# The first chunk of four down projections computed with seven products instead of eight, and both such chunks at a new place among the pairs

## The chip, the cores and the metric

The kernel runs on one core of a Trainium2 chip. The metric is the device time of one execution in microseconds; smaller is better. Engines are called as in the profile: PE (TensorE matmul), PEld (its weight load), DVE (VectorE), ACT (ScalarE), POOL (GpSimd) and SP (SyncE, which here only issues DMAs).

## What is computed

A two-layer encoder on 512 tokens of width 1024, all in float32. Each layer is a gated feed-forward block, a mixer (attention of several kinds), a cross attention to a memory, and a second feed-forward block. The change touches the four feed-forward blocks alone (`ffn1` and `ffn2` of both layers):

```python
def swiglu(x, wg, wu, wd):
    return (jax.nn.silu(x @ wg) * (x @ wu)) @ wd

h = h + 0.5 * swiglu(rmsnorm(h, g), wg, wu, wd)      # wg, wu: 1024 x 2816, wd: 2816 x 1024
```

## The kernel before

Everything is held transposed: features on the 128 partitions, tokens along the free axis. The hidden width of 2816 is 22 blocks of 128, taken as 11 **pairs** of blocks, numbered 0 to 10. A float32 matrix product is made of three matmuls: each operand is parted into a high and a low float32r part (ACT writes the high part with a copy, DVE the low part with a subtraction), and high x high, high x low and low x high are summed in PSUM. "Operand" below is this pair of instructions (`operand`, lines 515 to 528; L526 is ACT's, L527 is DVE's).

**A pair's gate and up projections** are done with a seven-product scheme of Strassen and Winograd instead of eight quarter products (pair 0 alone is done plainly). The weights of a pair are four quarters of 128 x 1024 elements (512 KB); sums and differences of quarters, and of token halves, give seven products of 24 matmuls of 128 x 256 each. The names are those of the token sums they use: "11", "1", "2", "21", "3", "4" and "22". Four functions emit them:

- `open_pair` (L559): product 11, from quarter 0 (tile `wf`).
- `sum_pair` (L578): products 1 and 2. Their weights are made in tile `s1` (three buffers): one quarter is loaded from SP (L584), a second is added to it in flight by an accumulating DMA that POOL issues (L585), and DVE then subtracts quarter 0 (L591).
- `cross_pair` (L600): product 21 from quarter 1 (`wf`), then product 3. The weights of product 3 are made in tile `s3`, which has **one buffer**: SP loads a quarter (L614), ACT negates it (L616), POOL issues an accumulating DMA that adds another quarter (L617), then ACT and DVE make the operand. When DVE has made the low part, the buffer is free and the next load into it can be issued.
- `close_pair` (L625): products 4 (`lower`) and 22 (`upper`, whose DVE subtraction is L637), and the gate: two DVE multiplications (L670, L673), a Silu on ACT (L672), and the high and low parts of the hidden values (L436, L440).

The loop in `ffn` emits `sum_pair(p)`, `cross_pair(p)`, `open_pair(p+1)`, `close_pair(p)`, so that PE runs 1, 2, 21, 3 of pair p, 11 of pair p+1, and 4, 22 of pair p.

Operand buffers are few: two for `wh`/`wl`, and one pair `sh`/`sl` that every third operand uses. `wf` has three buffers.

**The down projection** goes over the hidden blocks in three chunks, `CHUNKS = (6, 8, 8)` blocks, that is pairs 0 to 2, 3 to 6 and 7 to 10. Its outputs are eight tiles of 128 x 512, kept in `f.sum`. Chunks 0 and 2 are plain (`down`, matmuls of 128 x 512 at L796): chunk 0 is emitted after `sum_pair(3)`, with eight weight loads of 384 KB, eight operands (L168, L170) and eight ACT copies into `f.sum` (L807). Chunk 1 is done with the seven-product scheme (`paired_down`, L703) after `cross_pair(7)`, in two halves (`s` = 0, 1) of seven products each, with its own tiles in the same buffers `wf`, `s1` and `s3` (L742 is the negation, L743 the accumulating DMA). It adds its results to `f.sum` with DVE (L710). What it needs of the hidden values, sums over token quarters, is made in the gate of each of its pairs (`hidden_sums`, L682: four subtractions at L686, and high and low parts at L695 and L696).

The gate of a pair is emitted at once, or put off until after the next pair's `sum_pair` (for p of 1, 2, 6 and 10).

PE's order is the order of the code. The order on the other engines is made by a scheduler when the kernel is built, with the operands at a high priority. Each queue, SP's and POOL's DMA issues among them, then runs strictly in that order.

Of the kernel before, what the change touches and what calls it, by code (L numbers as in the profile page):

```python
# [70 lines left out]
CHUNKS = (6, 8, 8)  # L71
PAIRED = 1

# [39 lines left out]
class Encoder:  # L113
    def __init__(self, tc, ctx, I):
        self.tc, self.nc, self.I = tc, tc.nc, I
        nc = self.nc
        pool = lambda name, bufs, **kw: ctx.enter_context(tc.tile_pool(name=name, bufs=bufs, **kw))
        self.const = pool("const", 1)
        self.xp = pool("xp", 1)
        self.wp = pool("wp", 2)  # L120
        self.ps = pool("ps", 4, space=PSUM)
        self.small = pool("small", 2)
        self.dram = pool("dram", 1, space=bass.MemoryType.DRAM)
        self.ident = self.const.tile([P, P], F32, name="ident")
        make_identity(nc, self.ident)
        self.identb = self.const.tile([P, P], BF, name="identb")
        nc.vector.tensor_copy(self.identb, self.ident)
# [10 lines left out]
        self.x = [None] * KB  # L138
        self.left = 0
# [43 lines left out]
    def xtile(self):  # L183
        return self.xp.tile([P, S], F32, name="x", tag="x", bufs=KB)

# [128 lines left out]
    def ffn(self, pre):  # L314


        with ExitStack() as ctx:
            pool = lambda name: ctx.enter_context(self.tc.tile_pool(name=pre + name, bufs=1))
            f = self.f = SimpleNamespace(pre=pre, ctx=ctx, hp=pool("h"), tp=pool("t"), H={}, n=0, taken=None, own=False, low=None, gate=None, spread=None, macc=None,
                                        G={n: [None] * (CHUNKS[PAIRED] // 2) for n in ("11", "21", "22", "1", "2", "3", "4")})  # L320
            R = self.plain_pair()
# [4 lines left out]
            for p in range(1, FB // 2):  # L326
                final = p == FB // 2 - 1
                self.sum_pair(pair)
                if f.gate is not None:
                    f.gate, gate = None, f.gate  # L330
                    gate(f.lowered)
                if p in ends and c != PAIRED:
                    self.down(c)
                    c += 1
                self.cross_pair(pair)
                if p == 2:
                    self.set_aside()
                if p in ends and c == PAIRED and p == ends[c]:
                    self.paired_down()
                    c += 1  # L340
                if final:
                    early = self.block(c, 0, True)
                    self.down_products(c, early, LEAD + REST, False)
                    self.close_pair(pair, True)
                    self.down(c, early)
                else:
                    old, pair = pair, self.open_pair(p + 1)
                    gate = self.close_pair(old, False)
                    if p <= 2 or p + 1 in ends:
# [69 lines left out]
    def hidden(self, p, gs, us):  # L419
# [95 lines left out]
    def operand(self, t, own=None):  # L515

        nc, f = self.nc, self.f
        if own is None:
            own = f.n % 3 == 2
            f.n += 1  # L520
        if own:
            h, l = self.own_tiles()
        else:
            h, l = [self.wp.tile([P, 1024 + WHOLE], F32R, name=n, tag=n, bufs=2)[:, o:o + 1024]
                    for n, o in (("wh", LINE), ("wl", LINE + STEP))]
        self.leading = nc.scalar.activation(h, t, AF.Copy)  # L526
# [11 lines left out]
    def raw_quarter(self, p, q):  # L538
        return self.fetch(self.wp.tile([P, 1024], F32, name="wf", tag="wf", bufs=3), p, q)

    def product(self, bank, w, xs, first, late=False):

        half = KB // 2
        ops = [(z, a, b, k) for z in range(2) for a, b in ((0, 0), (0, 1), (1, 0)) for k in range(half)]
        if late:
            ops.sort(key=lambda op: op[3] == half - 1)
        for n, (z, a, b, k) in enumerate(ops):
            o = z * 512 + k * P
            self.nc.tensor.matmul(bank[:, z * 256:z * 256 + 256], w[a][:, o:o + P], xs[k][b],  # L549
# [75 lines left out]
    def close_pair(self, pair, final):  # L625
# [40 lines left out]
        def gates(after=None):  # L666
# [6 lines left out]
            nc.vector.tensor_mul(two(gs), two(t), gu[:, :, 1, :])  # L673
            j = p - sum(CHUNKS[:PAIRED]) // 2
            if 0 <= j < CHUNKS[PAIRED] // 2:
                self.hidden_sums(p, j, gs, t)
            else:
                self.hidden_parts(p, gs, 0)

        return gates  # L680

    def hidden_sums(self, p, j, h, t):  # L682

# [6 lines left out]
        sub(part(t, 2), part(h, 2), part(t, 1))  # L690
        self.hidden_parts(p, h, 0)
        two = [f.hp.tile([P, S], F32R, name=n, tag="T", bufs=CHUNKS[PAIRED]) for n in ("th", "tl")]
        one = [self.xs[j][c][:, 256:512] for c in range(2)]
        for src, (hi, lo) in ((t[:, 0:512], two), (part(t, 2), one)):
            nc.scalar.activation(hi, src, AF.Copy)  # L695
            nc.vector.tensor_sub(lo, src, hi.bitcast(F32))  # L696
        whole = f.H[p]
        for name, tiles, i in (("11", whole, 0), ("1", whole, 1), ("21", whole, 2), ("22", whole, 3),
                               ("3", two, 0), ("2", two, 1)):
            f.G[name][j] = tuple(part(x, i) for x in tiles)  # L700
        f.G["4"][j] = tuple(one)

    def paired_down(self):  # L703

        nc, f = self.nc, self.f

        def add(s, b, half, bank):
            for z in range(2):
                o = f.sum[4 * s + 2 * b + z][:, half * 256:half * 256 + 256]
                nc.vector.tensor_add(o, o, bank[:, z * 256:z * 256 + 256])  # L710

        for s in range(2):
            p, late = -s, s == 0
            y = self.bank("pa")
# [13 lines left out]
            add(s, 1, 1, z)  # L728
            with self.tc.high_priority():
                nc.vector.tensor_sub(t, t, w11)  # L730
# [7 lines left out]
            add(s, 0, 0, x)  # L738
# [15 lines left out]
            self.product(y, w, f.G["4"], False)  # L754
            add(s, 1, 0, y)

    def set_aside(self):
# [10 lines left out]
        f.sum = [self.xtile() for _ in range(KB)]  # L768
        self.x = [None] * KB
# [30 lines left out]
    def down(self, c, first=None):  # L800
# [16 lines left out]
        if last:  # L817
            kept = []
            for d in range(KB):
                kept.append(f.hp.tile([P, S], F32, name="kept", tag="T", bufs=CHUNKS[PAIRED]))  # L820
                with self.behind(self.loaded):
# [580 lines left out]
    def mem_stats(self, p):  # L1402
# [370 lines left out]
def _layout(inp):  # L1773
# [28 lines left out]
    for l in (0, 1):  # L1802
        pre = "l%d_" % l
        for f in ("ffn1_", "ffn2_"):
# [62 lines left out]
```

## Time and profile before

| | us |
|---|---|
| median of three runs | 2036.51 (2034.72 to 2036.95) |
| the profiled execution | 2033.43 |
| its span in the trace | 2031.7 |
| PE busy | 2019.3 |
| DVE busy | 1531.1 |
| ACT busy | 1239.7 |
| POOL busy | 337.6 |

The four feed-forward blocks lie at about 9 to 346, 709 to 1038, 1038 to 1367 and 1698 to 2032 us of the span. In the rows of the trace a line is `engine line operation out<-in`; buffer numbers are left out, so both `s1` and `s3` read `s` there, and L617 or L743 tells `s3`, L585 or L725 `s1`. A matmul's own duration includes time in which the next one already runs, so the pace of PE is read from how many matmuls start in a stretch. The chain of waits is the chain of work that ended last, followed back from the end.

### The profile page before, as it was taken

The numbers are of one execution on the slowest core, as the hardware profiler recorded it, in microseconds if no ns is written. First come the engines' busy times: TensorE is split into PE (matmuls) and PEld (weight loads), VectorE is DVE, ScalarE is ACT, GpSimd is POOL, SyncE is SP. The second block draws the span as 40 slices with busy tenths as digits, with TensorE's granted clock in tenths as the row PEclk, the third lists the DMA queues.
The fourth block names the chain that finished last, engine by engine and source line by source line (L and its number), as shares of the span: only waits on it lengthen the run. The fifth ranks groups of instructions, "written<-read, shape, count | busy, mean of one in ns | idle before, by whom it ended". The sixth has DMA issues, their size and how long they took to land.

```text
span 2031.7 us, 34101 instructions
## 1 busy us (share of the span) xinstructions
PE 2019.3 (99%) x13421; PEld 1833.6 (90%) x13421; DVE 1531.1 (75%) x2285; ACT 1239.7 (61%) x1891; POOL 337.6 (17%) x321
## 2 busy tenths in 40 slices
PE   9999999999999999999999999999999999999999
PEld 7999998888888898999989999988888888999997
DVE  8679776799676794897677597864668688759784
ACT  7566564556785574665655565745768566656572
POOL 1021001345521110100010000003353111000000
PEclk9999999999999999999999999999999999999999
DMA  7667754222331185776456577644223324757762
GB/s 236 172 181 183 199 167 159 99 85 86 97 127 63 63 247 157 179 185 188 147 175 197 158 198 194 178 132 139 93 83 126 103 73 143 215 158 198 190 178 93
DMA packets 98800, 307.00 MB, mean 151 GB/s; under 512 B 11088, under 2 KB 14288, under 8 KB 98640
## 3 DMA queue, kind: packets, MB, share of 16 engines
q1 hardware_dynamic: 84528, 253.97, 37.6%
q0 software_dynamic: 13824, 50.34, 14.2%
q8 instruction: 105, 1.72, 0.3%
q10 hardware_dynamic: 288, 0.52, 0.1%
q14 instruction: 55, 0.45, 0.1%
HBM read 292.21 MB, written 12.58 MB: 150 GB/s over the span
## 4 chain that ended last, share of the span: by engine, by line
PE 94%; DVE 2%; DMA 1%; ACT 1%; issue 1%; POOL 0%; SPq 0%; DVEq 0%; ACTq 0%; POOLq 0%
PE ps_pa L549 30%; PE ps_pa L919 13%; PE ps_pb L549 12%; PE ps_pa L796 8%; PE ps_pb L796 8%; PE ps_pa L865 5%; PE ps_pa L393 3%; PE ps_pb L1032 3%; PE ps_pa L1522 2%; PE ps_pa L1353 2%; PE ps_pb L865 2%; PE ps_pb L1085 1%; PE ps_pb L1058 1%; PE ps_pb L393 1%; PE ps_pa L1252 1%
## 5 line engine op out<-in xcount | busy, mean ns | idle before, releaser
L168 ACT ACTIVATE wh<-wf 128x1024 fp32r<-128x1024 f32 (+2 forms) x187 | 181.6, 977 | 248.2 <-PE ps_pb L796 52.8
L170 DVE TENSOR_TENSOR wl<-wf,wh 128x1024 fp32r<-128x1024 f32 (+2 forms) x144 | 161.7, 1127 | 94.0 <-ACT wh L168 92.0
L527 DVE TENSOR_TENSOR wl<-s,wh 128x1024 fp32r<-128x1024 f32 x132 | 161.4, 1224 | 67.3 <-ACT wh L526 65.5
L526 ACT ACTIVATE wh<-s 128x1024 fp32r<-128x1024 f32 x132 | 140.0, 1062 | 107.2 <-PE ps_pa L549 31.1
L527 DVE TENSOR_TENSOR wl<-wf,wh 128x1024 fp32r<-128x1024 f32 x96 | 116.8, 1220 | 30.1 <-ACT wh L526 30.0
L617 POOL DMA_DIRECT2D s<-l_ffn_wq x40 | 34.9, 873 | 602.6 <-ACT s L616 345.0
L526 ACT ACTIVATE wh<-wf 128x1024 fp32r<-128x1024 f32 x96 | 101.4, 1059 | 50.7 <-PE ps_pa L549 22.1
L170 POOL TENSOR_TENSOR wl<-wf,wh 128x1024 fp32r<-128x1024 f32 (+1 forms) x43 | 95.0, 2209 | 185.6 <-ACT wh L168 123.4
L919 PE MATMUL ps_pa<-wh,xh 128*128 128x512 f32 x384 | 121.8, 398 | 0.0
L919 PE MATMUL ps_pa<-wh,xl 128*128 128x512 f32 x384 | 118.9, 391 | 0.0
L919 PE MATMUL ps_pa<-wl,xh 128*128 128x512 f32 x384 | 118.7, 390 | 0.0
L526 ACT ACTIVATE sh<-s 128x1024 fp32r<-128x1024 f32 x60 | 63.7, 1061 | 50.9 <-PE ps_pa L549 18.0
L527 DVE TENSOR_TENSOR sl<-s,sh 128x1024 fp32r<-128x1024 f32 x60 | 73.3, 1222 | 27.4 <-ACT sh L526 26.9
L919 PEld LDWEIGHTS ps_pa<-wh,xl 128*128 128x128 f32 x384 | 72.1, 188 | 15.7
L919 PEld LDWEIGHTS ps_pa<-wl,xh 128*128 128x128 f32 x384 | 72.0, 188 | 15.6
L1047 ACT ACTIVATE e<-e,m 128x128 f32<-128x128 f32 (+3 forms) x128 | 70.7, 554 | 21.6 <-DVE m L1046 21.4
L585 POOL DMA_DIRECT2D s<-l_ffn_wq x40 | 35.8, 895 | 285.4 <-DMA s<-l_ffn_wq 240.5
L919 PEld LDWEIGHTS ps_pa<-wh,xh 128*128 128x128 f32 x384 | 69.1, 188 | 12.5 <-DVE vp L964 0.3
L549 PE MATMUL ps_pa<-xh,wh 128*128 128x256 f32 x480 | 74.1, 276 | 0.0
L549 PE MATMUL ps_pa<-xl,wh 128*128 128x256 f32 x480 | 74.0, 276 | 0.0
L549 PE MATMUL ps_pa<-xh,wl 128*128 128x256 f32 x480 | 74.0, 276 | 0.0
L526 ACT ACTIVATE sh<-wf 128x1024 fp32r<-128x1024 f32 x48 | 50.8, 1059 | 36.5 <-PE ps_pa L549 16.9
(460 smaller groups left out, 6037.7 us busy)
## 6 DMA issues: line engine op xcount, KB each, us to landing
wf<-l_ffn_wq SPq DMA_DIRECT2D x120, 512.0 KB, 4.4
s<-l_ffn_wq SPq DMA_DIRECT2D x80, 512.0 KB, 4.3
s<-l_ffn_wq POOLq DMA_DIRECT2D x80, 512.0 KB, 7.6
wf<-l_w_in SPq DMA_DIRECT2D x48, 512.0 KB, 3.5
wf<-l_ffn_wd SPq DMA_DIRECT2D x32, 512.0 KB, 3.7
wf<-l_ffn_wd SPq DMA_DIRECT2D x32, 384.0 KB, 3.5
wf<-l_ffn_wdq SPq DMA_DIRECT2D x24, 512.0 KB, 4.5
s<-l_ffn_wdq SPq DMA_DIRECT2D x16, 512.0 KB, 4.0
```

Of the source, the lines that this page charges most:

```text
L168: self.leading = nc.scalar.activation(wh[:, sl], w[:, sl], AF.Copy)
L170: eng.tensor_sub(wl[:, sl], w[:, sl], wh.bitcast(F32)[:, sl])
L393: nc.tensor.matmul(p, w[a][:, k * P:(k + 1) * P], xs[k][c], start=k == order[0] and a == c == 0, stop=k == order[-1] and a == 1)
L526: self.leading = nc.scalar.activation(h, t, AF.Copy)
L527: self.parted = nc.vector.tensor_sub(l, t, h.bitcast(F32))
L549: self.nc.tensor.matmul(bank[:, z * 256:z * 256 + 256], w[a][:, o:o + P], xs[k][b], start=first and n == 0, stop=n == len(ops) - 1, skip_g ...
L796: self.nc.tensor.matmul(bank, w[a][:, j * P:(j + 1) * P], h, start=j == a == e == 0 and c < len(CHUNKS) - 1, stop=j == nb - 1 and (a, e) = ...
L865: nc.tensor.matmul(banks[dd], w[g, k // 2][a][:, o:o + P], parts(k)[b], start=k == first and a == b == 0, stop=k == last and a == 1)
L919: nc.tensor.matmul(banks[j], xs[k][a][:, j * P:(j + 1) * P], w[b][:, kk * 512:kk * 512 + 512], start=k == a == b == 0, stop=k == KB - 1 an ...
L1032: nc.tensor.matmul(bank[:, o:o + n], a, b[:, :n], start=c == 0, stop=c == len(ops) - 1)
L1047: nc.scalar.activation(e, e, AF.Exp, bias=m[:, i:i + 1], scale=-1.0, accum_out=rs[:, i:i + 1])
L1353: nc.tensor.matmul(banks[c][i], a[:, i * P:(i + 1) * P], b[:, c * 512:(c + 1) * 512], start=(k == 0 and n == 0), stop=(k == KB - 1 and n = ...
```

## The change

`PAIRED` becomes `(0, 1)`: chunk 0 is done by `paired_down` too, with matrices of 768 columns instead of 1024 and products of 18 matmuls of 128 x 256. Its first contribution to each output is copied by ACT instead of added by DVE; the other contributions, of both chunks, are added by one DVE instruction over two outputs, for which the tiles of `f.sum` become halves of tiles of 1024 columns. The hidden values of pairs 0, 1 and 2 now need the sums of `hidden_sums` too. `paired_down(c)` is no longer emitted after `cross_pair`, but one pair later, after `sum_pair` of the pair that follows: chunk 0 after `sum_pair(4)`, chunk 1 after `sum_pair(8)`. The gates that are put off are now those of pairs 1, 2, 3 and 7, and the gates of 3 and 7 come behind the paired chunk. In the last pair the operand of product 4 is put behind an operand of the last chunk.

```diff
-PAIRED = 1
+PAIRED = (0, 1)
...
     def xtile(self):
-        return self.xp.tile([P, S], F32, name="x", tag="x", bufs=KB)
+        if self.xroom is None:
+            self.xroom = self.xp.tile([P, 2 * S], F32, name="x", tag="x", bufs=KB // 2)
+            return self.xroom[:, :S]
+        room, self.xroom = self.xroom, None
+        return room[:, S:]
...
                 self.sum_pair(pair)
+                if c in PAIRED and p == ends[c] + 1:
+                    self.paired_down(c)
+                    c += 1
                 if f.gate is not None:
                     f.gate, gate = None, f.gate
                     gate(f.lowered)
-                if p in ends and c != PAIRED:
+                if p in ends and c not in PAIRED:
                     self.down(c)
                     c += 1
                 self.cross_pair(pair)
...
-                if p in ends and c == PAIRED and p == ends[c]:
-                    self.paired_down()
-                    c += 1
                 if final:
                     early = self.block(c, 0, True)
+                    f.ahead = self.leading
...
-                    if p <= 2 or p + 1 in ends:
+                    if p <= 2 or p in ends:
                         f.gate = gate
...
+    def hidden_done(self, p, h, t, later=False):
+
+        for c in PAIRED:
+            j = p - sum(CHUNKS[:c]) // 2
+            if 0 <= j < CHUNKS[c] // 2:
+                return self.hidden_sums(p, j, h, t, later)
+        self.hidden_parts(p, h, 0, later)
...
     def product(self, bank, w, xs, first, late=False):
 
-        half = KB // 2
+        half = len(xs)
...
-                w = self.operand(self.raw_quarter(p, 3), own)
+                w = self.raw_quarter(p, 3)
+                with self.behind(f.ahead):
+                    w = self.operand(w, own)
...
-    def paired_down(self):
+    def paired_down(self, c):
...
-        def add(s, b, half, bank):
-            for z in range(2):
-                o = f.sum[4 * s + 2 * b + z][:, half * 256:half * 256 + 256]
-                nc.vector.tensor_add(o, o, bank[:, z * 256:z * 256 + 256])
+        n = CHUNKS[c] * P
+
+        def add(s, b, half, bank, first=False):
+            o = self.halves(f.rooms[2 * s + b])[:, :, half * 256:half * 256 + 256]
+            if first and c == 0:
+                nc.scalar.copy(o, self.halves(bank))
+            else:
+                nc.vector.tensor_add(o, o, self.halves(bank))
...
-                t = f.tp.tile([P, 1024], F32, name="s1", tag="s1", bufs=3)
+                t = f.tp.tile([P, 1024], F32, name="s1", tag="s1", bufs=3)[:, :n]
...
-                v = f.tp.tile([P, 1024], F32, name="s3", tag="s3", bufs=1)
+                v = f.tp.tile([P, 1024], F32, name="s3", tag="s3", bufs=1)[:, :n]
```

Two places show what the scheduler made of it; both are in the second feed-forward block, and the other three blocks have the same order there. The first is SP's queue. Before, in the second half of the paired chunk 1 (its loads are those from `wdq`), up to the next load into the buffer `s3`:

```order
L535 DMA wf_10076<-l0_ffn2_wdq 128x1024
L535 DMA s3_10108<-l0_ffn2_wdq 128x1024
L535 DMA s1_10310<-l0_ffn2_wq 128x1024
L535 DMA wf_10173<-l0_ffn2_wdq 128x1024
L535 DMA wf_10206<-l0_ffn2_wq 128x1024
L535 DMA wf_10239<-l0_ffn2_wq 128x1024
L535 DMA s3_10402<-l0_ffn2_wq 128x1024
```

Now, in the second half of the paired chunk 0 (from `wdq0`):

```order
L550 DMA wf_9171<-l0_ffn2_wdq0 128x768
L550 DMA s3_9196<-l0_ffn2_wdq0 128x768
L550 DMA s1_9471<-l0_ffn2_wq 128x1024
L550 DMA wf_9247<-l0_ffn2_wdq0 128x768
L550 DMA wf_9291<-l0_ffn2_wq 128x1024
L550 DMA wf_9357<-l0_ffn2_wq 128x1024
L550 DMA s3_9322<-l0_ffn2_wq 128x1024
```

The two queues look alike, but what stands between the two `s3` products on PE differs: before, `s3_10402` belonged to pair 8, and products 22 and 4 of the chunk, 11 of pair 8, 4 and 22 of pair 7, and 1, 2 and 21 of pair 8 lay between; now `s3_9322` belongs to pair 4, whose product 3 comes after 22 and 4 of the chunk and 21 of pair 4.

The second place is DVE's queue in the same half. Before, from the subtraction for product 2 (L730) to the low part of the `s3` operand:

```order
L730 TENSOR_TENSOR s1_10012<-s1_10012,wf_9979 128x1024
L710 TENSOR_TENSOR x_8342<-x_8342,ps_pa_9751 128x256
L710 TENSOR_TENSOR x_8343<-x_8343,ps_pa_9751 128x256
L527 TENSOR_TENSOR sl_10047<-s1_10012,sh_10046 128x1024
L748 TENSOR_TENSOR s1_10012<-wf_10076,s1_10012 128x1024
L527 TENSOR_TENSOR wl_10079<-wf_10076,wh_10078 128x1024
L710 TENSOR_TENSOR x_8346<-x_8346,ps_pb_10011 128x256
L710 TENSOR_TENSOR x_8347<-x_8347,ps_pb_10011 128x256
L527 TENSOR_TENSOR wl_10113<-s3_10108,wh_10112 128x1024
```

Now, from the same subtraction (L765) to the low part of `s3_9196` and the low parts behind it:

```order
L765 TENSOR_TENSOR s1_9121<-s1_9121,wf_9094 128x768
L542 TENSOR_TENSOR wl_9149<-s1_9121,wh_9148 128x768
L542 TENSOR_TENSOR wl_9174<-wf_9171,wh_9173 128x768
L783 TENSOR_TENSOR s1_9121<-wf_9171,s1_9121 128x768
L655 TENSOR_TENSOR s1_8853<-wf_9291,s1_8853 128x1024
L542 TENSOR_TENSOR sl_9201<-s3_9196,sh_9200 128x768
L542 TENSOR_TENSOR wl_9225<-s1_9121,wh_9224 128x768
```

New in it is L655, the subtraction for product 22 of pair 4. It reads `wf_9291`, which takes the buffer of `wf_9094` that L765 was the last to read, and it stands ahead of the low part of the `s3` operand.

More of the change, by code (lines that the diff above doesn't have):

```diff
@@ L318, in ffn @@
             pool = lambda name: ctx.enter_context(self.tc.tile_pool(name=pre + name, bufs=1))
-            f = self.f = SimpleNamespace(pre=pre, ctx=ctx, hp=pool("h"), tp=pool("t"), H={}, n=0, taken=None, own=False, low=None, gate=None, spread=None, macc=None,
-                                        G={n: [None] * (CHUNKS[PAIRED] // 2) for n in ("11", "21", "22", "1", "2", "3", "4")})
+            f = self.f = SimpleNamespace(pre=pre, ctx=ctx, hp=pool("h"), tp=pool("t"), H={}, n=0, taken=None, own=False, low=None, gate=None, ahead=None, spread=None, macc=None,
+                                        G=[])
             R = self.plain_pair()
@@ L547, in product @@
         for n, (z, a, b, k) in enumerate(ops):
-            o = z * 512 + k * P
+            o = (z * half + k) * P
             self.nc.tensor.matmul(bank[:, z * 256:z * 256 + 256], w[a][:, o:o + P], xs[k][b],
@@ L673, in gates, with hidden_sums @@
             nc.vector.tensor_mul(two(gs), two(t), gu[:, :, 1, :])
[L674 to L678, printed above, removed]
+            self.hidden_done(p, gs, t)
         return gates
-    def hidden_sums(self, p, j, h, t):
+    def hidden_sums(self, p, j, h, t, later):
         nc, f = self.nc, self.f
@@ L690, in hidden_sums, with low, both @@
         sub(part(t, 2), part(h, 2), part(t, 1))
-        self.hidden_parts(p, h, 0)
-        two = [f.hp.tile([P, S], F32R, name=n, tag="T", bufs=CHUNKS[PAIRED]) for n in ("th", "tl")]
+        self.hidden_parts(p, h, 0, later)
+        two = [f.hp.tile([P, S], F32R, name=n, tag="T", bufs=max(CHUNKS)) for n in ("th", "tl")]
         one = [self.xs[j][c][:, 256:512] for c in range(2)]
-        for src, (hi, lo) in ((t[:, 0:512], two), (part(t, 2), one)):
+        parts = ((t[:, 0:512], two), (part(t, 2), one))
+        for src, (hi, lo) in parts:
             nc.scalar.activation(hi, src, AF.Copy)
-            nc.vector.tensor_sub(lo, src, hi.bitcast(F32))
+        def low(after=None):
+            with self.behind(after):
+                for src, (hi, lo) in parts:
+                    nc.vector.tensor_sub(lo, src, hi.bitcast(F32))
+        if later:
+            first = f.low
+            def both(after=None):
+                first(after)
+                low(after)
+            f.low = both
+        else:
+            low()
+        if j == 0:
+            f.G = {name: [] for name in ("11", "21", "22", "1", "2", "3", "4")}
         whole = f.H[p]
@@ L767, in set_aside @@
                     nc.sync.dma_start(kept[d], self.x[d])
-        f.sum = [self.xtile() for _ in range(KB)]
+        f.rooms, f.sum = [], []
+        for d in range(KB):
+            f.sum.append(self.xtile())
+            if d % 2 == 0:
+                f.rooms.append(self.xroom)
         self.x = [None] * KB
@@ L819, in down @@
             for d in range(KB):
-                kept.append(f.hp.tile([P, S], F32, name="kept", tag="T", bufs=CHUNKS[PAIRED]))
+                kept.append(f.hp.tile([P, S], F32, name="kept", tag="T", bufs=max(CHUNKS)))
                 with self.behind(self.loaded):
@@ L1413, in mem_stats @@
                 if k % 2 == 0:
-                    two = f.hp.tile([P, S], F32, name="mem", tag="T", bufs=CHUNKS[PAIRED])
+                    two = f.hp.tile([P, S], F32, name="mem", tag="T", bufs=max(CHUNKS))
                 m = two[:, k % 2 * NMEM:k % 2 * NMEM + NMEM]
@@ L1809, in _layout @@
             out[pre + f + "wd"] = wd = blocks(a[pre + f + "wd"])
-            n0 = sum(CHUNKS[:PAIRED])
-            wd = wd.reshape(2, 2, 2, P, FB, P)[:, :, :, :, n0:n0 + CHUNKS[PAIRED]].reshape(2, 2, 2, P, KB // 2, 2, P)
-            out[pre + f + "wdq"] = np.ascontiguousarray(wd.transpose(0, 1, 5, 3, 2, 4, 6)).reshape(2, 4, P, 1024)
+            for c in PAIRED:
+                size, start = CHUNKS[c], sum(CHUNKS[:c])
+                w = wd.reshape(2, 2, 2, P, FB, P)[:, :, :, :, start:start + size].reshape(2, 2, 2, P, size // 2, 2, P)
+                out[pre + f + "wdq%d" % c] = np.ascontiguousarray(w.transpose(0, 1, 5, 3, 2, 4, 6)).reshape(2, 4, P, size * P)
         for g in ("mix_norm", "mem_norm", "mem_src_norm"):
```

30 lines of the change are left out of this document (17 added, 13 removed).

## The prediction

> **What bounds the kernel now.** I read the page's busy rows and the shares of the chain of waits first, then the chain in order of time in the second feed-forward block, then PE's waits.
>
> ```profile
> span 2031.7 us, 34101 instructions
> PE 2019.3 (99%) x13421; PEld 1833.6 (90%) x13421; DVE 1531.1 (75%) x2285; ACT 1239.7 (61%) x1891; POOL 337.6 (17%) x321
> PE 94%; DVE 2%; DMA 1%; ACT 1%; issue 1%; POOL 0%; SPq 0%; DVEq 0%; ACTq 0%; POOLq 0%
> ```
>
> PE is the bound: 94% of the chain, and it is idle for about 12 us of the span. Its pace stands in the chain, first for a plain chunk's output, then for products of pairs and of chunk 1:
>
> ```profile
> 786.26 4.08 PE ps_pa L796 x18
> 806.66 4.08 PE ps_pb L796 x18
> ...
> 910.03 5.44 PE ps_pa L549 x48
> 918.19 8.16 PE ps_pa L549 x72
> ```
>
> Eighteen matmuls of 128x512 take 4.08 us, 226.7 ns each; 48 of 128x256 take 5.44 us, 113.3 ns each. Half the columns cost half the time, so that the change's products don't pay is excluded by these rows. A product of 24 takes 2.72 us, a pair 19.04. PE is at full pace, so only fewer matmuls can gain, and each new wait is lost in full. The waits of PE that lie where the change works are few:
>
> ```profile
> PE ps_pa L549 <- DVE wl L527: 2.5, 4, 0.7
> PE ps_pa L549 <- DVE hl L440: 1.6, 3, 1.1
> PE ps_pa L549 <- ACT wh L526: 0.6, 1, 0.6
> ```
>
> L527 is the operand of product 2 of pair 6, L440 the hidden values of pair 6, for which the chunk right behind had to wait.
>
> **The matmuls.** Chunk 0 before: 8 outputs of 18 matmuls, 8 x 4.08 = 32.64 us. Now: 14 products of 18 matmuls of 128x256, 14 x 18 x 0.1133 = 28.56 us. That is −4.08 in each feed-forward block, **−16.3** in all.
>
> **The old waits.** Chunk 1 no longer follows pair 6 at once: a pair and two more products stand between them. L440's 1.6 us should go, and L527's 2.5 with it, since product 2 of pair 6 doesn't share DVE with the same rush. Each such wait is followed by less than a microsecond of refill in PE's start times; I take 4.1 plus 0.9, **−5.0**. L526's is left out.
>
> **The `s3` loop** is what speaks against the change. One buffer serves every "3" operand, and the next load goes out when DVE has read the last one. Before, from the second half of chunk 1 to pair 8 (the columns of a row are start, duration, engine, line, operation):
>
> ```profile
> 912.30 1.22 DVE L730 TENSOR_TENSOR s<-s,wf 128x1024 f32<-128x1024 f32 x1
> 916.00 1.22 DVE L748 TENSOR_TENSOR s<-wf,s 128x1024 f32<-128x1024 f32 x1
> 917.14 1.22 DVE L527 TENSOR_TENSOR wl<-wf,wh 128x1024 fp32r<-128x1024 f32 x1
> 918.94 1.22 DVE L527 TENSOR_TENSOR wl<-s,wh 128x1024 fp32r<-128x1024 f32 x1
> 920.18 3.04 SPq L535 DMA_DIRECT2D s<-l_ffn_wq  x2
> 923.89 1.06 ACT L616 ACTIVATE s<-s 128x1024 f32<-128x1024 f32 x1 [2.28 <-DMA s<-l_ffn_wq]
> 925.24 0.86 POOL L617 DMA_DIRECT2D s<-l_ffn_wq  x1 [14.93 <-ACT s L616]
> 931.37 1.06 ACT L526 ACTIVATE wh<-s 128x1024 fp32r<-128x1024 f32 x1 [1.66 <-PE ps_pa L549]
> 932.50 1.22 DVE L527 TENSOR_TENSOR wl<-s,wh 128x1024 fp32r<-128x1024 f32 x1
> ```
>
> The low part ends at 920.16, the load is issued at 920.18, the negation follows, the accumulating DMA goes out 0.29 us after its end, and the operand is ready 13.5 us after the load. Nobody waited, since eight products lay between the chunk's product 3 and pair 8's. How long the steps take elsewhere (landing of the accumulating DMA for pairs; for chunk 1; here; then median landings of plain loads):
>
> ```profile
> DMA to landing us min/median/max: 5.5/6.7/13.8
> DMA to landing us min/median/max: 5.9/7.4/8.2
> DMA to landing us min/median/max: 5.5/5.5/5.5
> s<-l_ffn_wq SPq DMA_DIRECT2D x80, 512.0 KB, 4.3
> wf<-l_ffn_wq SPq DMA_DIRECT2D x30, 512.0 KB, 4.7
> wf<-l_ffn_wq SPq DMA_DIRECT2D x3, 512.0 KB, 6.0
> ```
>
> Release to high part: load 4.3, gap 0.08, negation 1.06, gap 0.29, accumulation 6.2 (between 5.5 here and the median 6.7), gap 0.10, high part 1.06: **13.1**. Bounds: 11.7 with the load of 3.7 seen here (920.18 to 923.89) and 5.5; 15.1 with 8.2. The low part is needed 0.9 us into the product (after eight matmuls) and follows 1.2 behind the high part: 0.35 more.
>
> *Pair 4's product 3.* Now only 22 and 4 of chunk 0 and 21 of pair 4 stand between the chunk's last product 3 and this one. From the start of the second half (11, 1, 2, 21, 3, 22, 4 of 2.04 each, then 21 of 2.72) it is due at 7 x 2.04 + 2.72 = 17.0 us. The release is late too: DVE has L655 ahead of the low part, and L655 waits for a `wf` whose buffer L765 frees. In the rows above the same subtraction (L730) ended 0.8 us after product 11 began (923.63, two products into the last row of the chain, less 10.88, is 912.75). With 0.7 here for the smaller form, a load of 5.4 (between 4.7 and 6.0), L655 1.22 and the low part 0.96, the release is at 8.3; bounds 7.2 (load of 4.4, DVE's rows 1.14 apart) and 9.3 (6.0 and an addition ahead). So 8.3 + 13.1 + 0.35 = 21.75, a wait of **4.75** (2.25 to 7.75).
>
> *Pair 8's product 3.* Its due time is 8 x 2.72 = 21.76. L765 ends at 0.8, the load lands at 6.2, then DVE has L655 1.14, another low part 1.14, an addition 0.6 and the `s3` low part 1.22: release at 10.3 (9.2 to 11.3). 10.3 + 13.1 + 0.35 = 23.75: a wait of **2.0** (0 to 5.0).
>
> What is queued behind: POOL's accumulating DMA stands idle for ACT, ACT's high part for the DMA; on PE, product 3, then 11 of the next pair, everything. In four blocks: 4 x 6.75 = **+27.0** (+9.0 to +51).
>
> **DVE, ACT and the queues.** Rows of the second block: the groups with the durations, then busy time by stretch (length, then PE, PEld, DVE, ACT, POOL, clock, DMA share, GB/s).
>
> ```profile
> L686 DVE TENSOR_TENSOR t<-gs 128x256 f32<-128x256 f32 x8 | 3.4, 420 | 0.1
> L170 DVE TENSOR_TENSOR wl<-wf,wh 128x768 fp32r<-128x768 f32 x8 | 7.6, 955 | 10.7 <-ACT wh L168 10.7
> L696 DVE TENSOR_TENSOR tl<-t,th 128x512 fp32r<-128x512 f32 x4 | 2.7, 685 | 0.0
> ...
> 738.00:757.00 19.00, 19.00 (x169) 19.00 (x169) 18.96 (x21) 12.41 (x14) 0.92 (x1) 1.00 0.82 268
> 757.00:776.00 19.00, 19.00 (x170) 19.00 (x170) 14.07 (x14) 12.38 (x15) 2.62 (x3) 1.00 0.85 211
> 778.00:811.00 33.00, 33.00 (x149) 27.36 (x148) 12.57 (x13) 13.60 (x20) 0.00 (x0) 1.00 0.45 139
> 893.00:931.00 38.00, 37.92 (x334) 37.73 (x333) 31.88 (x46) 19.98 (x22) 4.34 (x5) 1.00 0.74 186
> ```
>
> Chunk 0 had 8 low parts, 7.6 us of DVE. It gets 14 (13.4), 4 subtractions of that size (3.8) and 4 additions of 512 elements (at L696's 0.685, 2.7): 20 us in 28.6. `hidden_sums` adds to each of the pairs 0, 1 and 2 four times 0.42 and about 0.7 for the low part: 2.4. Chunk 1 ran well with DVE at 31.88 of 38 (84%); 20 plus pair 4's operands is near that. ACT has 14 high parts for 8, and 8 copies as before, with half of its time free. SP issues 10 loads of 384 KB for 8 and POOL 4 accumulating DMAs, so 14 x 384 KB for 8 x 384: 2.3 MB more in a stretch where DMA engines were 45% busy. All of this lies under PE's 28.6 us, **0** in the sum; the cover fails first at 738 to 757, where DVE has no free time now (a rival, below). The gates of pairs 3 and 7, now behind the chunk, are wanted a pair or more later: 0. In the last pair the operand behind chunk 2's one is also 0, for its product follows that chunk's first outputs.
>
> **The sum.** −16.3 − 5.0 + 27.0 = +5.7 on the profiled execution's 2033.4: 2039.1. The median of the runs shown, 2036.5, is 3.1 above that execution, so I forecast **2042** (2024 to 2066 by the bounds alone).
>
> **The rivals.**
>
> *The loop fits better than that.* With the release at 7.2 and 5.5 for the accumulation, pair 4 waits 2.25 and pair 8 nothing: −21.3 + 9.0 = −12.3, **2024**. For it: all three accumulations at 890 to 930 took 5.5, beside DMA engines at 74%. Against it: medians of 6.7 and 7.4 over all, and the chunk's extra transfers, which use the same engines just there. This case holds the time of 2020 to 2033, and takes the other side.
>
> *DVE is late in pairs 1 to 3.* At 738 to 757 it is busy 18.96 of 19 us, and 2.4 and more come on top for each of the pairs 0 to 2. The next stretch has 4.9 free, so a pair late by 2.4 recovers; it decides if the late instruction is an operand (these have the high priority) and not the gate. If one pair's 2.4 shows on PE in full in each block, +9.6: **2052**.
>
> *PE's clock falls after the new waits.* The trace shows PE slow once, at the start (then the row of the first 4 us):
>
> ```profile
> 1.63 4.87 PE L223 MATMUL ps_pb<-warm,identb 128*128 128x512 bf16 x11 [1.63 <-DVE identb L127]
> 0.00:4.00 4.00, 2.37 (x6) 0.89 (x7) 0.70 (x4) 1.47 (x2) 0.70 (x6) 1.00 0.48 152
> ```
>
> Eleven matmuls in 4.87 us are 443 ns each against 226.7 later, and the granted clock's column reads 1.00 even there. Later idle times are about 1 us and cost no pace. If a wait of 4.75 us sets PE back to that state, it loses half of 4.87, 2.4 us, once per block: +9.7, **2052**; it decides at a length of idle somewhere between 1.1 and 4.75 us. [...]
>
> **How the numbers follow.** Forecast 0.44 (own range 2031 to 2052), the loop that fits 0.29, DVE 0.13, the clock 0.14. A measurement tells 0.2%, 4.1 us, from no change: faster is below 2032.4, slower above 2040.6. Faster: 0.25 of the second case, 0.02 of the first, 0.01 of others: 0.28. Same: 0.18, 0.04 and 0.04: 0.26. Slower: the rest, 0.46. The range is 2024 to 2056: below it a fifth of the fast case, above it the clock or DVE on top of a longer loop.
>
> **What would show it.** PE's waits should have product 3 (L565) waiting for ACT's high or DVE's low part, four times about 4.7 us before pair 4's and four times about 2 before pair 8's. `s3`'s load, negation and accumulation should be in the chain, and L655 should wait for a `wf` load in the second half of both chunks. The rows of L440 and L527 should be gone, and the 14 products of chunk 0 take 28.6 us. The forecast is wrong if PE goes through product 3 of pair 4 without stopping, if the wait there is under 2 us, if matmuls behind a wait start 227 ns apart where 113 is the pace, or if the time is lost in pairs 1 to 3.

## The result, and the profile after

| | before | changed |
|---|---|---|
| median, us | 2036.59 (2034.72 to 2036.95) | 2055.38 (2053.63 to 2057.78) |
| profiled execution, us | 2033.43 | 2055.4 |
| ratio, 95% interval | | 1.0099 (1.0087 to 1.0111) |

The change is 18.8 us slower; 5.5 were forecast. From the page of the changed kernel, its span, busy rows and the shares of the chain of waits:

```profile
span 2053.6 us, 35258 instructions
PE 2016.1 (98%) x13849; PEld 1846.8 (90%) x13853; DVE 1592.4 (78%) x2363; ACT 1279.1 (62%) x1955; POOL 357.4 (17%) x339
PE 85%; DMA 6%; issue 3%; DVE 3%; ACT 3%; POOL 0%; SPq 0%; ACTq 0%; DVEq 0%; POOLq 0%
```

The span is 21.9 us longer. PE's share of the chain fell from 94% to 85%, and DMA's rose from 1% to 6%. What PE waited for (us in total, times, longest):

```profile
PE ps_pa L565 <- ACT wh L541: 13.9, 8, 2.7
PE ps_pa L565 <- DVE sl L542: 4.8, 4, 1.3
PE ps_pa L835 <- ACT sh L169: 2.8, 4, 0.7
PE ps_pa L565 <- DVE wl L542: 2.3, 4, 0.6
PE ps_pa L565 <- ACT gu L638: 2.1, 3, 1.1
```

The eight waits of the first row are product 3 of pairs 4 and 8 in the four blocks (L541 makes the high and L542 the low part of an operand). The chain of waits in the second block, in order of time, shows the loop from the release to that product:

```profile
827.71 0.96 DVE sl L542
828.69 3.43 DMA s<-l_ffn_wq
832.19 1.07 ACT s L632
833.55 5.45 DMA s<-l_ffn_wq
839.08 1.07 ACT wh L541
840.17 1.24 DVE wl L542
```

DVE's low part ends, SP's load into `s3` starts at once, ACT negates, POOL's accumulating DMA lands, ACT makes the high part and DVE the low part. On DVE the release was late (timeline):

```profile
822.25 0.95 DVE L783 TENSOR_TENSOR s<-wf,s 128x768 f32<-128x768 f32 x1
826.56 1.23 DVE L655 TENSOR_TENSOR s<-wf,s 128x1024 f32<-128x1024 f32 x1 [3.36 <-DMA wf<-l_ffn_wq]
827.71 0.95 DVE L542 TENSOR_TENSOR sl<-s,sh 128x768 fp32r<-128x768 f32 x1
```

DVE stood still for 3.36 us at L655, for a load that took 7.2 us (819.32 to 826.54). It did so in the second half of both chunks in all four blocks, as its row among DVE's waits says (us in total, times, longest):

```profile
DVE s L655 <- DMA wf<-l_ffn_wq: 22.3, 8, 3.5
```

PE's timeline at the same place (the last bracket is the idle time before the row and what ended it):

```profile
828.71 0.62 PE L565 MATMUL ps_pa<-th,sl 128*128 128x256 f32 x3 [1.17 <-DVE sl L542]
840.19 0.74 PE L565 MATMUL ps_pa<-t3h,wh 128*128 128x256 f32 x4 [2.56 <-ACT wh L541]
841.45 0.74 PE L565 MATMUL ps_pa<-t3h,wl 128*128 128x256 f32 x4
```

The chunk's own product 3 waits first, for the low part behind L655; then pair 4's.

**The account.** From the starts of all matmuls I took the time between neighbours less the columns at full pace (0.4427 ns each: 4.08 us for 18 matmuls of 512); what is left over is lost time. Summed by product over the four blocks, changed kernel less before:

| | us |
|---|---|
| matmuls saved | −16.3 |
| chunk 0's product 3, and products 21 and 3 of pair 4 | +22.4 |
| the same at chunk 1 and pair 8, and product 21 of chunk 1 | +11.0 |
| last chunk's first block (L835) | +4.2 |
| product 4 of pair 7 (behind ACT's L638) | +3.1 |
| product 3 of pairs 5 and 9, and one product 4 | +2.5 |
| waits of before: product 2 of pairs 5 and 6, hidden values of pair 6 | −7.7 |
| product 2, now of pair 7 (one 0.3 of pair 5) | +3.0 |
| sum | +22.2 |

against +21.9 of the span.

### The profile page after: what moved, and what is told of

It reads as the page before. It is cut to its first block, busy times and chain, and to the rows that moved or that the text cites. A ratio compares the mean times of both kernels' runs of the same rounds, so it can differ in the third digit from the quotient of the medians.

```text
span 2053.6 us, 35258 instructions
## 1 busy us (share of the span) xinstructions
PE 2016.1 (98%) x13849; PEld 1846.8 (90%) x13853; DVE 1592.4 (78%) x2363; ACT 1279.1 (62%) x1955; POOL 357.4 (17%) x339
## 2 busy tenths in 40 slices
DMA packets 102263, 316.53 MB, mean 154 GB/s; under 512 B 11472, under 2 KB 14672, under 8 KB 102096
## 4 chain that ended last, share of the span: by engine, by line
PE 85%; DMA 6%; issue 3%; DVE 3%; ACT 3%; POOL 0%; SPq 0%; ACTq 0%; DVEq 0%; POOLq 0%
PE ps_pa L565 28%; PE ps_pa L958 13%; PE ps_pb L565 12%; PE ps_pa L904 5%; PE ps_pa L835 4%; PE ps_pb L835 4%; DMA s<-l_ffn_wq 4%; PE ps_pa L399 3%; PE ps_pb L1071 3%; PE ps_pa L1561 2%; PE ps_pa L1392 2%; PE ps_pb L904 2%; PE ps_pb L1124 1%; PE ps_pb L1097 1%; DMA s<-l_ffn_wdq 1%
## 5 line engine op out<-in xcount | busy, mean ns | idle before, releaser
L169 ACT ACTIVATE wh<-wf 128x1024 fp32r<-128x1024 f32 (+1 forms) x155 | 154.4, 1003 | 177.6 <-issue 37.8
L542 DVE TENSOR_TENSOR wl<-s,wh 128x1024 fp32r<-128x1024 f32 (+1 forms) x140 | 167.3, 1197 | 71.9 <-ACT wh L541 70.2
L541 ACT ACTIVATE wh<-s 128x1024 fp32r<-128x1024 f32 (+1 forms) x140 | 145.1, 1036 | 120.7 <-DMA s<-l_ffn_wq 42.0
L541 ACT ACTIVATE wh<-wf 128x1024 fp32r<-128x1024 f32 (+1 forms) x124 | 125.9, 1016 | 65.3 <-PE ps_pa L565 41.7
L171 DVE TENSOR_TENSOR wl<-wf,wh 128x1024 fp32r<-128x1024 f32 (+1 forms) x110 | 128.7, 1175 | 41.8 <-ACT wh L169 39.8
L542 DVE TENSOR_TENSOR wl<-wf,wh 128x1024 fp32r<-128x1024 f32 (+1 forms) x124 | 144.4, 1167 | 10.1 <-ACT wh L541 10.0
L541 ACT ACTIVATE sh<-s 128x1024 fp32r<-128x1024 f32 (+1 forms) x84 | 85.7, 1020 | 49.4 <-PE ps_pb L565 15.4
L542 DVE TENSOR_TENSOR sl<-s,sh 128x1024 fp32r<-128x1024 f32 (+1 forms) x84 | 98.2, 1169 | 20.9 <-ACT sh L541 19.6
L565 PE MATMUL ps_pa<-xh,wh 128*128 128x256 f32 x528 | 82.2, 277 | 0.0
L565 PE MATMUL ps_pa<-xl,wh 128*128 128x256 f32 x528 | 82.1, 276 | 0.0
L565 PE MATMUL ps_pa<-xh,wl 128*128 128x256 f32 x528 | 82.1, 276 | 0.0
L632 ACT ACTIVATE s<-s 128x1024 f32<-128x1024 f32 x40 | 42.5, 1063 | 54.8 <-DMA s<-l_ffn_wq 51.3
```

Of the source, the lines that this page charges most:

```text
L169: self.leading = nc.scalar.activation(wh[:, sl], w[:, sl], AF.Copy)
L171: eng.tensor_sub(wl[:, sl], w[:, sl], wh.bitcast(F32)[:, sl])
L542: self.parted = nc.vector.tensor_sub(l, t, h.bitcast(F32))
L632: nc.scalar.activation(s, s, AF.Copy, scale=-1.0)
```

## The experiments

Ratios are to the kernel before on the same chip (medians 2034.3 to 2035.1). The theory: PE waits for the loop through the single `s3` buffer, set off by L655. Rivals: the transfers limit this stretch whatever the order, or DVE has too much work.

**e1: L655 behind pair 4's own `s3` operand.**

```diff
-            with self.tc.high_priority(), self.behind(f.crossed if p == 1 else None):
+            with self.tc.high_priority(), self.behind(f.crossed if p in (1, 4, 8) else None):
```

> Edit: in pairs 4 and 8 the subtraction for product 22 (L655) is issued after the low part of the pair's own s3 operand, so it no longer stands on DVE ahead of the low part of the paired chunk's second s3 operand. Theory (s3 loop, set off by L655): that low part then follows its high part (high part at 822.5 in the trace of the changed kernel, low part 824.3 instead of 828.7), the waits at the chunk's own product 3 go (8.1 us in all), and pair 4's product 3 is ready 5.8 + 11.6 + 0.35 = 17.75 us after the half's start against 17.0 due: 0.75 left in each block; pair 8's wait goes. 2055.4 - 27 = 2028, faster than before. Rival (the transfers are the limit: the load of pair 4's quarter 1 lands late because the chunk's transfers fill the DMA engines): the wait moves to products 21 and 22 of pair 4, 2045 or more. Rival (DVE has too much work): 2050 or more.

Measured 2036.85, ratio 1.0008 (0.9999 to 1.0018): 18.5 us gained, 27 expected. The waits at the chunk's own product 3 and at pair 8 are gone. Pair 4's stayed; the row of PE's waits, and then ACT's and POOL's timeline in the second block:

```profile
PE ps_pa L565 <- ACT wh L541: 11.8, 4, 4.0
```

```profile
818.42 1.06 ACT L632 ACTIVATE s<-s 128x1024 f32<-128x1024 f32 x1 [1.41 <-DMA s<-l_ffn_wq]
819.78 0.86 POOL L633 DMA_DIRECT2D s<-l_ffn_wq  x1 [12.47 <-DMA s<-l_ffn_wq]
827.62 1.06 ACT L541 ACTIVATE wh<-s 128x1024 fp32r<-128x1024 f32 x1 [5.33 <-DMA s<-l_ffn_wq]
```

The release came 5.8 us after the half's start, as expected, but from it to the high part's end the loop took 15.3 us: the load 4.9 for 3.4 and the accumulation 7.8 for 5.4. So the place of L655 sets the release and is worth 18 us net of that, and the loop's length isn't a constant.

**e2: own room for the second half's operand.**

```diff
-                v = f.tp.tile([P, 1024], F32, name="s3", tag="s3", bufs=1)[:, :n]
+                v = f.tp.tile([P, 1024], F32, name="s3", tag="t" if s else "s3", bufs=1)[:, :n]
```

> Edit: the s3 operand of the second half of each paired chunk takes the room of the gate's tile t (free until the gate that follows the chunk), so pair 4's and pair 8's s3 load waits only for the first half's operand. Theory (s3 loop): the waits at product 3 of pairs 4 and 8 go (14.0 and 7.8 us of the changed kernel's 32.4), those at the chunk's own product 3 stay (8.1, since L655 is still ahead of its low part): 2055.4 - 21.8 = 2034. Rival (transfers): with more loads open at once they only land later, 2045 or more. Rival (DVE): no change, 2055.

Measured 2033.56, ratio 0.9994 (0.9985 to 1.0004); 2034 was expected.

```profile
PE ps_pa L565 <- DVE sl L542: 5.5, 4, 2.1
PE ps_pa L835 <- ACT sh L169: 2.8, 4, 0.7
```

The 13.9 us of waits for ACT's high part are gone, and those at the chunk's own product 3, behind L655, remain. With the same products, transfers and DVE work, the single buffer is shown to be the cause of the larger part: 21.8 us between the two medians, waits and clock together.

**e3: both chunks at chunk 1's old place.**

```diff
-                if c in PAIRED and p == ends[c] + 1:
-                    self.paired_down(c)
-                    c += 1
 ...
                 if p == 2:
                     self.set_aside()
+                if c in PAIRED and p == ends[c]:
+                    self.paired_down(c)
+                    c += 1
 ...
-                    if p <= 2 or p in ends:
+                    if p <= 2 or p + 1 in ends:
```

> Edit: both chunks 0 and 1 with seven products, but each at the place where chunk 1 was before (behind the products 21 and 3 of the pair whose number is the chunk's end: 3 and 7), with the gates put off as before. Theory (s3 loop): eight products again lie between a chunk's last s3 product and the next pair's, so no wait behind the chunk; in front of chunk 0 only 11, 1, 2, 21 of 2.04 us lie between pair 3's product 3 and the chunk's first (10.9 us for a loop of about 13): 0 to 3 us in each block. 2036.6 - 16.3 + 6 = 2026 (2020 to 2032). Rivals (transfers, DVE): the seven products themselves are the load, 2045 or more wherever they stand.

Measured 2044.77, ratio 1.0052 (1.0037 to 1.0068): a miss. No product 3 of the loop waited, as the theory has it, but each chunk's first product waited for the hidden values of the pair just before it, 2.9 us a block at chunk 0 (3.7 in the last) and 2.4 at chunk 1 in lost time. PE's timeline at chunk 0:

```profile
787.08 0.39 PE L565 MATMUL ps_pa<-hh,wh 128*128 128x256 f32 x1 [1.00 <-ACT hh L450]
788.79 0.39 PE L565 MATMUL ps_pa<-hl,wh 128*128 128x256 f32 x1 [1.32 <-DVE hl L454]
```

The new place does remove a wait, then; it put one on `s3` instead.

**e4: e1 and e2, and the rotation of the operands' buffers one step on.**

```diff
-            f = self.f = SimpleNamespace(pre=pre, ctx=ctx, hp=pool("h"), tp=pool("t"), H={}, n=0,
+            f = self.f = SimpleNamespace(pre=pre, ctx=ctx, hp=pool("h"), tp=pool("t"), H={}, n=1,
```

> Edits of the first two runs together, and the rotation that gives every third operand the single pair sh/sl is started one step on, so that in the last pair product 21 uses it and not product 3, right behind which the last chunk's first block wants it. Theory: all of the loop's waits (32.4 us with the clock's part) and the four waits of 0.86 us at L835 (4.2) go: 2055.4 - 36.6 = 2019, with 3 to 5 us of small waits elsewhere perhaps: 2019 to 2025. Rivals (transfers, DVE): above 2040.

Measured 2032.55, ratio 0.9988 (0.9979 to 0.9998): 13.6 us above the 2019 expected. The waits of the loop and of L835 are gone, but the new rotation gave blocks 2 and 4 a wait at their start:

```profile
PE ps_pb L418 <- DVE factor L405: 8.9, 3, 4.3
```

```profile
735.00:739.00 4.00, 4.00 (x24) 4.00 (x24) 4.00 (x6) 3.70 (x5) 0.00 (x0) 0.63 0.28 113
```

The second fence is the stretch behind the 4.3 us wait: the granted clock (the third number from the end) is 0.63 there.

**e5: the rotation moved on only behind chunk 0.** e1 and e2, and at the end of `paired_down`:

```diff
+        if c == 0:
+            f.n += 1
```

> The own room of e2 and the order of L655 of e1, and the rotation of sh/sl moved on by one only behind chunk 0, so that the start of a block is as in the changed kernel (in e4 the first products of blocks 2 and 4 waited 4.5 us at L418, and the clock's column fell to 0.63 behind it). Theory (s3 loop, and each wait paid in full): e4's 2032.6 less two of those waits with what follows (4.7 + 1.8 and about as much): 2019.5 (2016 to 2023). Rival (the transfers set the limit, the waits only move): the gain is under 5 us, 2028 or more.

Measured 2025.50, ratio 0.9951 (0.9938 to 0.9965): faster than before, 6 us short. Pair 4's product 21 waits 1.2 us in each block for its low part, which stands on DVE behind the gate of pair 3:

```profile
822.64 1.22 DVE L454 TENSOR_TENSOR hl<-gs,hh 128x1024 fp32r<-128x1024 f32 x1
824.37 0.69 DVE L715 TENSOR_TENSOR tl<-t,th 128x512 fp32r<-128x512 f32 x1
824.97 1.22 DVE L542 TENSOR_TENSOR wl<-wf,wh 128x1024 fp32r<-128x1024 f32 x1
```

**e6: chunk 1 at its new place, chunk 0 plain.**

```diff
-PAIRED = (0, 1)
+PAIRED = (1,)
 ...
-                    if p <= 2 or p in ends:
+                    if p <= 2 or p == 7:
```

> Edit against the changed kernel: chunk 0 plain again (eight outputs), chunk 1 with seven products at its new place, gate of pair 7 put off, gate of pair 3 not. Theory (s3 loop): the loop's waits at chunk 1 and pair 8 (2.2 + 7.8 us in the changed kernel, some 2 of it the clock) come, the waits of before at chunk 1's first product (2.9 in all) go: 2035.1 + 7 = 2042. Rival (the new place is good for chunk 1 and only chunk 0 costs): 2032.

Measured 2047.49, ratio 1.0062 (1.0048 to 1.0075). Moving chunk 1 alone costs 13 us, not 7. Its row is

```profile
PE ps_pa L565 <- ACT wh L541: 7.9, 5, 2.1
```

and the slower clock behind some of these waits (0.998 granted in the mean of the execution) comes on top.

**e7: two more negations in the loop.**

```diff
                 nc.scalar.activation(s, s, AF.Copy, scale=-1.0)
+            if p in (4, 8):
+                nc.scalar.activation(s, s, AF.Copy, scale=-1.0)
+                nc.scalar.activation(s, s, AF.Copy, scale=-1.0)
```

> Edit: in pairs 4 and 8 the s3 quarter is negated three times instead of once: two ACT instructions of 1.06 us more in the loop, about 2.2 us, before the accumulating DMA goes out. The values are the same. Theory (s3 loop is what PE waits for): eight waits longer by 2.2 us each, +17.6, and with waits of about 5 us in front of pair 4's product 3 the granted clock falls behind more of them than the two seen in the changed kernel, 1.3 to 2.3 us each: 2055.4 + 17.6 + 2 to 6 = 2077. Rivals (transfers, DVE): the loop has slack, under 2060.

Measured 2110.37, ratio 1.0371 (1.0352 to 1.0390): 55 us more than the changed kernel for 22 expected. The wait's row, the loop's accumulation in the chain, and the stretch of the product behind one wait and the one after it:

```profile
PE ps_pa L565 <- ACT wh L541: 61.3, 8, 10.2
```

```profile
847.39 8.58 DMA s<-l_ffn_wq
```

```profile
857.00:862.20 5.20, 5.10 (x24) 5.10 (x25) 2.36 (x2) 1.43 (x3) 0.00 (x0) 0.52 0.32 104
862.20:866.00 3.80, 3.80 (x36) 3.80 (x35) 2.06 (x3) 3.40 (x5) 0.86 (x1) 1.00 0.21 60
```

The loop has no slack. At this place 3.0 us came from ACT and 3.1 more because the accumulation, sent later, took 8.58 us for 5.45. Behind all eight waits (6.5 to 10.4 us) one product of 24 ran at a clock near 0.5 (0.52 in the first of the two stretches above, 1.00 in the next) and lost 2.3 to 2.5 us.

**e8: e5 without e1's order of L655.** The edits of e2 and of e5's rotation.

> As e5 without the order of L655: own room, rotation moved on behind chunk 0. Theory: the waits at the chunk's own product 3 stay, since DVE has L655 ahead of its low part (1.3 to 1.6 us a block, more in the second), and the four waits at L835 go: e2's 2033.6 - 4.2 = 2029. If e5 is no faster than this, the place of L655 does not matter once the buffer is free.

Measured 2040.58, ratio 1.0028 (1.0018 to 1.0039): 12 us over the expectation and 15 behind e5. L835's waits went, but product 21 of pair 4 lost 2.8 us a block: the rotation gave it other buffers, and with L655 early its low part stood behind the gate even later (PE's timeline):

```profile
831.73 0.74 PE L565 MATMUL ps_pa<-xh,wl 128*128 128x256 f32 x4 [1.42 <-DVE wl L542]
```

So the place of L655 matters with a free buffer too.

**e9: e5, and the gates of pairs 3 and 7 later.**

```diff
-                if f.gate is not None:
+                if f.gate is not None and p not in (4, 8):
                     f.gate, gate = None, f.gate
                     gate(f.lowered)
 ...
                 self.cross_pair(pair)
+                if f.gate is not None:
+                    f.gate, gate = None, f.gate
+                    gate(f.crossed)
```

> e5, and the gates of pairs 3 and 7 stand behind products 21 and 3 of pairs 4 and 8 instead of ahead of them. In e5 the low part of pair 4's product 21 stood on DVE behind that gate's high and low parts (L454, L715), and PE waited 1.24 us for it in each block. Theory (DVE's added work costs only where one of its instructions stands ahead of an operand): 2025.5 - 4 x 1.37 = 2020, unless the gate now stands ahead of products 4 and 22. Rival (DVE simply has too much work in this stretch): the wait moves on, 2025.

Measured 2018.04, ratio 0.9915 (0.9900 to 0.9930): 17 us faster than before, some 37 faster than the changed kernel. From its page, and its longest waits beside the one at the start:

```profile
span 2014.9 us, 35276 instructions
PE 2002.0 (99%) x13853; PEld 1839.5 (91%) x13853; DVE 1596.6 (79%) x2363; ACT 1280.0 (64%) x1955; POOL 357.0 (18%) x339
```

```profile
PE ps_pa L568 <- DVE wl L545: 3.1, 4, 1.1
PE ps_pa L402 <- ACT xh L233: 0.7, 1, 0.7
```

DVE has the 2363 instructions of the changed kernel and as much busy time (1596.6 us for 1592.4). Its total work is not what cost time; the order on it was. The transfers are those of the changed kernel as well (316.53 MB in both).

**e10: e1 without pair 6's and pair 10's accumulation.** These pairs' weights for products 1, 2 and 22 then lack a quarter.

```diff
-            nc.gpsimd.dma_start(pair.s, self.quarter(p, 2), accum_op=OP.add)
+            if p not in (6, 10):
+                nc.gpsimd.dma_start(pair.s, self.quarter(p, 2), accum_op=OP.add)
```

> e1 without the accumulating DMA (L601) of pairs 6 and 10, so their weights for products 1, 2 and 22 lack one quarter: that part of the computation is left out. In e1 this DMA of pair 6 went out 0.53 us behind pair 4's accumulation into s3, which then took 7.76 us to land (5.45 in the changed kernel). Theory (two accumulations at a time slow each other): pair 4's lands in 5.5, its waits of 2.2 to 4.1 us get 2.3 shorter and the clock no longer falls behind them: 2036.9 - 4 x 2.3 - 4 = 2024. Rival (the plain loads from SP slow it): 2036.

Measured 2034.84, ratio 1.0000 (0.9990 to 1.0011). The wait's row, and the landing of pair 4's accumulation in the second block:

```profile
PE ps_pa L565 <- ACT wh L541: 10.6, 4, 3.6
```

```profile
DMA to landing us min/median/max: 7.5/7.5/7.5
```

It still took 7.5 us with no second accumulation behind it. So the second accumulation is not what made e1's take 7.8. The rival's 2036 fits the time, but this run doesn't test whether the plain loads slow it.

**e11: chunk 0 as changed, chunk 1 at its old place.**

```diff
-                if c in PAIRED and p == ends[c] + 1:
+                if c == 0 and p == ends[c] + 1:
 ...
+                if c == 1 and p == ends[c]:
+                    self.paired_down(c)
+                    c += 1
 ...
-                    if p <= 2 or p in ends:
+                    if p <= 3 or p + 1 in ends:
```

> Only chunk 0 as in the changed kernel (seven products, behind products 1 and 2 of pair 4, gate of pair 3 put off); chunk 1 with seven products where it was before. The other half of e6. Theory (the loop's waits of each chunk stand alone): -16.3 for the matmuls, + 23 for chunk 0's part of the loop with the clock, + 4.2 at L835, the old waits stay: 2034.3 + 11 = 2045. With e6's +13 the two halves should be near the whole's +19, more by the old waits that e6 takes away.

Measured 2050.96, ratio 1.0072 (1.0055 to 1.0089).

```profile
PE ps_pa L568 <- ACT wh L544: 10.2, 4, 2.8
PE ps_pa L568 <- ACT hh L453: 3.6, 4, 1.2
PE ps_pa L568 <- DVE hl L457: 3.5, 4, 0.9
```

The loop's four waits are those of pair 4. The halves, +15.9 here and +13.2 in e6, add to more than the whole's 18.8, because chunk 1's wait for pair 6's hidden values grew here, to 9.4 us of lost time from 2.9 before, and the new place takes it away. e3 lost the same 2.4 us a block there with chunk 0 at another place, so it doesn't hang on that place; why it grew isn't settled.

## Why the prediction was right in its cause and wrong in its size

The span grew by 21.9 us where the sum said 5.7. Two things failed. Waits that the sum put at 0 or had no term for cost 9.8 us, and the `s3` loop cost 6.4 us more than its term. (Between the medians the miss is 13.3 us, 18.8 for 5.5, since the profiled execution of before was 3.1 us under its median and that of the changed kernel at its own.) The measured 2055.4 still lies inside the stated range, 0.6 us under its upper end, which stood for the clock or DVE on top of a longer loop; most of the excess is neither.

*Cause and place: right.* Product 3 of pairs 4 and 8 waits for the `s3` loop in all four blocks (e2), and L655 holds the release (e1, and e5 beside e8).

*Matmuls, −16.3: right.* The nominal time fell by that.

*Pair 4, 4.75 a block: measured 5.6.* In the second block 5.13: the product itself 3.2, product 21 of pair 4 0.5 and the chunk's product 3 1.45. The step "the release is at 8.3" failed: it was at 10.1 (828.67 against a half that began at 818.54; 10.1 to 10.3 in all four blocks), since L655's load took 7.2 us where I took 5.4. The step after it erred the other way: 11.5 us (828.69 to 840.15) for my 13.1. The sum of the two was right by chance, and I had not seen that so late a low part stops the chunk's own product 3 first. In the fourth block the clock adds 1.3.

*Pair 8, 2.0 a block: measured 2.75.* Three blocks lost 1.7, 1.7 and 2.2 us, near the forecast. The first lost 5.5: there the release was at 11.4 for the 10.3 forecast, the load took 5.9 us for 4.3, and the clock added 1.4. The loop as a whole: +33.4 for +27.0; 2.7 of the 6.4 are the clock.

*Old waits, −5.0: measured −4.7*, but not by the step given, so the size is luck. Pair 6's hidden values no longer hold PE up. Product 2's wait did not go; it moved from pair 6 to pair 7.

*What the sum left out: +9.8.* "The gates of pairs 3 and 7 ... 0" overlooked the other side of that edit: the gate of pair 6 is no longer put off. ACT's timeline of the changed kernel shows its high parts (L450, L710) ahead of the copy that pair 7's product 4 waits for:

```profile
902.57 1.07 ACT L450 ACTIVATE hh<-gs 128x1024 fp32r<-128x1024 f32 x1
903.53 0.62 ACT L710 ACTIVATE th<-t 128x512 fp32r<-128x512 f32 x1
904.05 0.41 ACT L710 ACTIVATE xh<-t 128x256 fp32r<-128x256 f32 x1
904.35 1.05 ACT L541 ACTIVATE wh<-s 128x1024 fp32r<-128x1024 f32 x1
905.30 0.57 ACT L638 COPY gu<-ps_pa 128x512 f32<-128x512 f32 x1
```

The wait is worth 3.1 us; that the gate makes it is read from this timeline and not shown by a run. In before, e3 and e11, which put that gate off, the product lost nothing, but there chunk 1 also stands ahead of it; and product 4 of pair 6, with pair 5's gate not put off either, lost nothing here. At pair 7 ACT has chunk 1's operands to make as well. 2.5 us more, product 3 of pairs 5 and 9 and one product 4, had no term either; the waits of pairs 5 and 9 are gone in e1 and e2, but what made them isn't shown.

And "In the last pair ... also 0" overlooked the rotation: every third operand uses `sh`/`sl`, chunk 0 brings 14 operands, and 14 leaves 2 over three. So pair 10's product 3 took the buffers that the last chunk's first block wants next, 4.2 us at L835; with the rotation moved on, these waits are gone in e4, e5, e8 and e9. The rotation could have been counted from the code.

So of the 16.5 us between +5.7 and +22.2, the loop's terms were 6.4 short, 9.8 had no term, and the old waits were 0.3 off.

*The rivals.* The loop that fits: no. Its one good premise, 5.5 us for the accumulation, held in pair 4 of all four blocks, and the time was lost at the release. DVE late in pairs 1 to 3: no wait of PE over 0.5 us there, and DVE's work is not the cause (e9). The clock: in part, once in four at pair 4 and once in four at pair 8; its 2.4 us is right once a wait is long (2.3 to 2.5 in e7), and it fell behind shorter waits than the forecast's at pair 4.

## What to carry to other kernels

When a step is moved, follow every single-buffered tile it uses to the next user, in units of what PE does in between, and look on the queue of the engine that frees the buffer for an instruction that waits for a load of its own. Count what a round-robin of buffers does when operands are added, and read an edited condition for what it stops doing too. The same products, with another room for one operand, the rotation moved on by one and L655 and two gates later (e9), turned 0.99% slower into 0.85% faster.

## What the runs showed of the hardware

PE's clock fell behind waits well inside the 1.1 to 4.75 us that the prediction left open. Windows of the changed kernel over product 3 behind waits of 2.73, 2.77 and 2.30 us (the clock is the third number from the end):

```profile
840.00:843.50 3.50, 3.25 (x25) 3.05 (x26) 3.31 (x3) 3.35 (x6) 0.00 (x0) 1.00 0.93 234
1838.40:1843.00 4.60, 4.53 (x25) 4.53 (x26) 3.59 (x3) 3.17 (x6) 0.00 (x0) 0.63 0.92 249
254.40:259.10 4.70, 4.57 (x25) 4.44 (x26) 4.09 (x4) 2.79 (x5) 0.00 (x0) 0.64 0.90 250
```

The length of the wait alone doesn't decide it: behind 2.73 us it stayed at 1.00 here, behind 2.30 us it fell, and in e6, where no wait is longer than 2.1 us, it fell behind 1.85. The changed kernel's trace has two falls inside its blocks, from 255.33 to 258.74 us and from 1839.11 to 1842.53, both to 0.50. Below are the two windows that the 2.73 us wait lies across, then the 3.41 us ahead of each fall and the fall itself, behind the 2.77 us wait and behind the 2.30 us one (the matmuls of a window stand behind the busy time):

```profile
835.62:839.03 3.41, 2.00 (x16) 1.81 (x16) 0.78 (x2) 0.00 (x0) 0.00 (x0) 1.00 0.92 174
839.03:842.44 3.41, 2.19 (x16) 1.99 (x17) 2.27 (x2) 3.36 (x5) 0.00 (x0) 1.00 0.96 250
1835.70:1839.11 3.41, 0.80 (x7) 0.64 (x6) 0.66 (x1) 1.75 (x2) 0.00 (x0) 1.00 1.01 217
1839.11:1842.53 3.42, 3.42 (x18) 3.42 (x18) 2.93 (x3) 2.16 (x4) 0.00 (x0) 0.50 0.93 244
251.92:255.33 3.41, 1.27 (x11) 1.08 (x10) 0.82 (x1) 1.91 (x2) 0.00 (x0) 1.00 0.97 210
255.33:258.74 3.41, 3.41 (x18) 3.28 (x17) 3.27 (x4) 1.51 (x3) 0.00 (x0) 0.50 0.90 252
```

Ahead of the two falls PE was busy for 0.80 and 1.27 us of 3.41; in the two windows over the wait without a fall it was busy for 2.00 and 2.19. So much was measured; what sets off a fall isn't shown by it.

An accumulating DMA of 512 KB took 5.3 to 5.6 us or 7.5 to 7.8 at the same place, and longer elsewhere (7.6 to 10.2 in pairs 4 and 8 of e7). In e1 pair 4's took 5.5, 7.8, 7.8 and 5.3 in the four blocks, in e10, with no second one behind it, 5.6, 7.5, 7.6 and 5.5. What decides between the two stays open.
